# LoRA router on one core: x as float32 on SyncE's queue and float32 transposes, in place of a converting load on GpSimd's queue

## Chip, core and metric

The kernel runs on one NeuronCore of a Trainium2 chip. The metric is the device time of one execution in microseconds (us); the median of the runs shown counts. The engines are named as the profile has them: PE (TensorE's matmuls), PEld (TensorE's weight loads), DVE (VectorE), ACT (ScalarE), POOL (GpSimd), SP (SyncE); SP, ACT and POOL also issue DMA transfers.

## What is computed

```python
batch, seq, dim, num_loras = 16, 512, 1024, 8      # x, router_weights: float32
logits = np.matmul(x, router_weights)
exp_logits = np.exp(logits - np.max(logits, axis=-1, keepdims=True))
return (exp_logits / np.sum(exp_logits, axis=-1, keepdims=True)).astype(np.float32)
```

There are 8192 rows of 1024 values (33.5 MB of float32), a projection of each row onto 8 columns, and a softmax over these 8. Reading x once is nearly all of the memory traffic.

## The kernel before

x is taken as 64 blocks (MO) of 128 consecutive rows; a block has one row per partition and KO = 8 pieces of 128 columns. For each block:

- L62: POOL issues a DMA that reads 512 KB of float32 and writes 256 KB of bf16 into `x_bf`; the conversion is made in the transfer. `x_bf` has 6 buffers (L52), so the issue for block j waits until the transposes of block j - 6 have read theirs.
- L72: eight transposes on PE, each with a weight load (the 128 x 128 piece of `x_bf`) and a matmul against the bf16 identity, into one PSUM tile `pt` (2 buffers).
- L73: DVE copies `pt` (128 x 1024 bf16) to `xT` in SBUF.
- L77: eight projections on PE accumulate 128 x 8 logits in PSUM, each with a weight load (a piece of `xT`).
- L84: DVE copies the logits to `logits_sb`.

After each 8 blocks (MB) the softmax follows on 128 x 64 values: maximum and subtraction on DVE (L87, L89), exponential on ACT (L96), sum, reciprocal and product on DVE (L98 to L102), and SP issues the store (L108). In the result eight consecutive float32 values belong to one row and the rows of a partition lie 128 rows apart, so a store of 32 KB is 1024 pieces of 32 bytes.

The order of the instructions on each engine is the scheduler's: on PE the transposes of block j + 1 stand ahead of the projections of block j. Before the loop the identity is built on POOL (L43) and the weights are loaded by SP and converted by DVE (L45, L50).

Of the kernel before, what the change touches and what calls it, by code (L numbers as in the profile page):

```python
# [1 line left out]

# [5 lines left out]


@with_exitstack  # L10
def kernel(
    ctx: ExitStack,
    tc: tile.TileContext,
    x: bass.AP,
    router_weights: bass.AP,
    out: bass.AP,
):
    nc = tc.nc
    P = 128
    B, S, D = x.shape  # L20
    D2, N = router_weights.shape
    assert D2 == D
    M = B * S
    assert D % P == 0
    KO = D // P
    assert M % P == 0
    MO = M // P

    MB = 8
    assert MO % MB == 0  # L30
    MG = MO // MB

    x_flat = x.rearrange("b s d -> (b s) d")
    out_flat = out.rearrange("b s n -> (b s) n")

    fp32 = mybir.dt.float32
    bf16 = mybir.dt.bfloat16
    Exp = mybir.ActivationFunctionType.Exp
    X = mybir.AxisListType.X

    const_pool = ctx.enter_context(tc.tile_pool(name="const", bufs=1))
    identity = const_pool.tile([P, P], bf16)
    make_identity(nc, identity)  # L43
    w_f32 = const_pool.tile([P, KO, N], fp32)
    nc.sync.dma_start(  # L45
        out=w_f32[:],
        in_=router_weights.rearrange("(ko ki) n -> ki ko n", ki=P),
    )
    w_tile = const_pool.tile([P, KO, N], bf16)
    nc.vector.tensor_copy(out=w_tile[:], in_=w_f32[:])  # L50

    sbuf = ctx.enter_context(tc.tile_pool(name="sbuf", bufs=6))  # L52
    sm_pool = ctx.enter_context(tc.tile_pool(name="sm", bufs=3))
    psum_l = ctx.enter_context(tc.tile_pool(name="psum_l", bufs=2, space=bass.MemoryType.PSUM))
    psum_t = ctx.enter_context(tc.tile_pool(name="psum_t", bufs=2, space=bass.MemoryType.PSUM))

    for mg in range(MG):
        logits_sb = sm_pool.tile([P, MB, N], fp32)
        for mb in range(MB):
            mo = mg * MB + mb  # L60
            x_bf = sbuf.tile([P, KO, P], bf16)
            nc.gpsimd.dma_start(  # L62
                out=x_bf[:],
                in_=x_flat[mo * P:(mo + 1) * P, :].rearrange(
                    "m (ko ki) -> m ko ki", ki=P
                ),
            )

            xT = sbuf.tile([P, KO, P], bf16)
            pt = psum_t.tile([P, KO, P], bf16)  # L70
            for ko in range(KO):
                nc.tensor.transpose(pt[:, ko, :], x_bf[:, ko, :], identity)  # L72
            nc.vector.tensor_copy(out=xT[:], in_=pt[:])  # L73

            logits = psum_l.tile([P, N], fp32)
            for ko in range(KO):
                nc.tensor.matmul(  # L77
                    logits,
                    lhsT=xT[:, ko, :],
                    rhs=w_tile[:, ko, :],  # L80
                    start=(ko == 0),
                    stop=(ko == KO - 1),
                )
            nc.vector.tensor_copy(out=logits_sb[:, mb, :], in_=logits)  # L84

        mx = sm_pool.tile([P, MB, 1], fp32)
        nc.vector.reduce_max(mx[:, :, 0], logits_sb[:], axis=X)  # L87
        sub = sm_pool.tile([P, MB, N], fp32)
        nc.vector.tensor_tensor(  # L89
            out=sub[:],  # L90
            in0=logits_sb[:],
            in1=mx[:].broadcast_to([P, MB, N]),
            op=mybir.AluOpType.subtract,
        )
        expv = sm_pool.tile([P, MB, N], fp32)
        nc.scalar.activation(expv[:], sub[:], func=Exp)  # L96
        sm = sm_pool.tile([P, MB, 1], fp32)
        nc.vector.reduce_sum(sm[:, :, 0], expv[:], axis=X)  # L98
        inv = sm_pool.tile([P, MB, 1], fp32)
        nc.vector.reciprocal(inv[:], sm[:])  # L100
        outv = sm_pool.tile([P, MB, N], fp32)
        nc.vector.tensor_tensor(  # L102
            out=outv[:],
            in0=expv[:],
            in1=inv[:].broadcast_to([P, MB, N]),
            op=mybir.AluOpType.mult,
        )
        nc.sync.dma_start(  # L108
            out=out_flat[mg * MB * P:(mg + 1) * MB * P, :].rearrange(
                "(mb p) n -> p mb n", p=P  # L110
            ),
            in_=outv[:],
        )


# [1 line left out]
_INS = ['x', 'router_weights']  # L117
_OUTS = [((16, 512, 8), 'float32')]


# [23 lines left out]
```

## Time and profile before

| | |
|---|---|
| time, three runs | 97.52, 96.8, 97.43 us; median 97.43 |
| span of the profiled execution | 95.1 us |
| own time of the profiled execution | not listed apart from the three runs; they lie 1.7 to 2.4 us above its span |
| mean granted TensorE clock | 0.642 |
| busy | PE 75.5, PEld 68.7, DVE 55.4, ACT 3.3, POOL 34.6 us |
| x's loads | 64 issues, 6.5 us (median) from issue to landing |
| stores | 8 issues, 13.2 us (median) from issue to landing, the queue in front of them included |
| chain that ended last | DMA 48%, PE 21%, issue 14%, POOL 9% of the span |

The span runs from the first to the last instruction of the profiled execution. The page cuts it into 40 slices of 2.4 us; each digit is the busy share in tenths, and in the row PEclk the clock that TensorE was granted, in tenths of full speed (9 also stands for full). A group of instructions is a line with its count, its busy time, the mean of one in ns, and behind the last bar the idle time of the engine ahead of these instructions and what ended most of it. In the timeline the columns are start, duration, engine, line, operation, output and inputs, and the count; the end of a matmul is modelled, so that a row of eight that ends at 58.91 has handed PE to the next instruction earlier.

### The profile page before, as it was taken

The numbers are of one execution on the slowest core, as the hardware profiler recorded it, in microseconds if no ns is written. First come the engines' busy times: TensorE is split into PE (matmuls) and PEld (weight loads), VectorE is DVE, ScalarE is ACT, GpSimd is POOL, SyncE is SP. The second block draws the span as 40 slices with busy tenths as digits, with TensorE's granted clock in tenths as the row PEclk, the third lists the DMA queues.
The fourth block names the chain that finished last, engine by engine and source line by source line (L and its number), as shares of the span: only waits on it lengthen the run. The fifth ranks groups of instructions, "written<-read, shape, count | busy, mean of one in ns | idle before, by whom it ended". The sixth has DMA issues, their size and how long they took to land.

```text
span 95.1 us, 2428 instructions
## 1 busy us (share of the span) xinstructions
PE 75.5 (79%) x1024; PEld 68.7 (72%) x1024; DVE 55.4 (58%) x169; ACT 3.3 (4%) x9; POOL 34.6 (36%) x70
## 2 busy tenths in 40 slices
PE   0048996579999999899998999899979997699500
PEld 0037985468888899788887888898879885698400
DVE  0023666647766765767556765586676657666630
ACT  5000000010001000000001000100001000100010
POOL 6922444424443334434344433344443345100000
PEclk9999999975555555555555555555555559655885
DMA  1799999999999999999999999999999999996001
GB/s 11 120 185 199 208 208 216 202 209 209 211 208 198 210 209 207 202 211 209 196 211 210 208 210 197 210 208 207 208 204 210 207 200 210 210 209 82 0 4 10
DMA packets 18586, 17.22 MB, mean 181 GB/s; under 512 B 10384, under 2 KB 10384, under 8 KB 18576
## 3 DMA queue, kind: packets, MB, share of 16 engines
q0 software_dynamic: 9216, 16.78, 95.2%
q1 hardware_dynamic: 9360, 0.30, 7.6%
q8 instruction: 8, 0.13, 0.5%
q14 instruction: 2, 0.02, 0.0%
HBM read 33.59 MB, written 0.26 MB: 356 GB/s over the span
## 4 chain that ended last, share of the span: by engine, by line
DMA 48%; PE 21%; issue 14%; POOL 9%; DVE 2%; POOLq 0%; ACT 0%; ACTq 0%
DMA x_bf<-in_x_dram 48%; PE pt L72 17%; POOL x_bf L62 9%; PE logits L77 4%; DVE xT L73 1%; POOL identity masks.py:199 0%; POOLq L62 0%; ACT expv L96 0%; DVE sub L89 0%; DVE sm L98 0%; DVE mx L87 0%; DVE outv L102 0%; DVE inv L100 0%; POOL identity masks.py:197 0%; DVE logits_sb L84 0%
## 5 line engine op out<-in xcount | busy, mean ns | idle before, releaser
L72 PE MATMUL pt<-identity,x_bf 128*128 128x128 bf16 x512 | 63.0, 300 | 12.9 <-DMA x_bf<-in_x_dram 11.4
L72 PEld LDWEIGHTS <-x_bf 128*128 128x128 bf16 x512 | 46.8, 135 | 17.9 <-DMA x_bf<-in_x_dram 13.5
L73 DVE COPY xT<-pt 128x1024 bf16<-128x1024 bf16 x64 | 44.1, 689 | 24.0 <-PE pt L72 23.5
L62 POOL DMA_DIRECT2D x_bf<-in_x_dram x64 | 34.0, 532 | 46.0 <-PE logits L77 35.5
L77 PEld LDWEIGHTS <-xT 128*128 128x128 bf16 x512 | 24.2, 111 | 3.1 <-DVE xT L73 2.4
L77 PE MATMUL logits<-w_tile,xT 128*128 128x8 bf16 x512 | 25.0, 172 | 1.4 <-DVE xT L73 1.4
L84 DVE COPY logits_sb<-logits 128x8 f32<-128x8 f32 x64 | 9.9, 154 | 8.6 <-PE logits L77 8.6
L96 ACT ACTIVATE expv<-sub 128x64 f32<-128x64 f32 x8 | 2.0, 256 | 86.8 <-DVE sub L89 86.8
L50 DVE CAST w_tile<-w_f 128x64 bf16<-128x64 f32 x1 | 0.2, 195 | 3.0 <-DMA w_f<-in_router_weights_dram 3.0
L98 DVE TENSOR_REDUCE sm<-expv 128x8 f32<-128x64 f32 x8 | 1.7, 210 | 0.4 <-ACT expv L96 0.4
L89 DVE TENSOR_TENSOR sub<-logits_sb,mx 128x64 f32<-128x64 f32 x8 | 1.8, 224 | 0.0
L102 DVE TENSOR_TENSOR outv<-expv,inv 128x64 f32<-128x64 f32 x8 | 1.8, 223 | 0.1
L87 DVE TENSOR_REDUCE mx<-logits_sb 128x8 f32<-128x64 f32 x8 | 1.7, 210 | 0.0
L100 DVE RECIPROCAL inv<-sm 128x8 f32<-128x8 f32 x8 | 1.6, 195 | 0.0
L96 ACT ACT_TABLE_LOAD x1 | 1.3, 1283 | 0.7 <-PEq L128 0.7
masks.py:199 POOL TENSOR_SCALAR_AFFINE_SELECT identity<-identity 128x128 bf16<-128x128 bf16 x1 | 0.3, 304 | 0.1
masks.py:197 POOL MEMSET identity<- 128x128 bf16 x1 | 0.2, 204 | 0.3 <-POOLq L128 0.3
L128 POOL MEMSET const-float32-0.0<- 128x1 f32 x1 | 0.1, 98 | 0.2 <-issue 0.2
L128 POOL MEMSET const-bfloat16-1.0<- 128x1 bf16 x1 | 0.1, 102 | 0.0
L128 POOL MEMSET const-uint8-127<- 128x1 uint8 x1 | 0.1, 102 | 0.0
L128 POOL MEMSET const-float32-1.0<- 128x1 f32 x1 | 0.1, 98 | 0.0
## 6 DMA issues: line engine op xcount, KB each, us to landing
x_bf<-in_x_dram POOLq DMA_DIRECT2D x64, 256.0 KB, 6.5
out_dram<-outv SPq DMA_DIRECT2D x8, 32.0 KB, 13.2
w_f<-in_router_weights_dram SPq DMA_DIRECT2D x1, 32.0 KB, 2.2
```

The lines of the kernel that those rows point to most:

```text
L62: nc.gpsimd.dma_start(out=x_bf[:], in_=x_flat[mo * P:(mo + 1) * P, :].rearrange("m (ko ki) -> m ko ki", ki=P),)
L72: nc.tensor.transpose(pt[:, ko, :], x_bf[:, ko, :], identity)
L73: nc.vector.tensor_copy(out=xT[:], in_=pt[:])
L77: nc.tensor.matmul(logits, lhsT=xT[:, ko, :], rhs=w_tile[:, ko, :], start=(ko == 0), stop=(ko == KO - 1),)
L84: nc.vector.tensor_copy(out=logits_sb[:, mb, :], in_=logits)
L87: nc.vector.reduce_max(mx[:, :, 0], logits_sb[:], axis=X)
L89: nc.vector.tensor_tensor(out=sub[:], in0=logits_sb[:], in1=mx[:].broadcast_to([P, MB, N]), op=mybir.AluOpType.subtract,)
L96: nc.scalar.activation(expv[:], sub[:], func=Exp)
L98: nc.vector.reduce_sum(sm[:, :, 0], expv[:], axis=X)
L100: nc.vector.reciprocal(inv[:], sm[:])
L102: nc.vector.tensor_tensor(out=outv[:], in0=expv[:], in1=inv[:].broadcast_to([P, MB, N]), op=mybir.AluOpType.mult,)
L128: nc = _bacc.Bacc("TRN2", target_bir_lowering=False, num_devices=1)
```

## The change

- x is loaded by SP as plain float32, 20 loads of 1, 1, 2, then 14 times 4, then 2, 1, 1 "rows"; a row here is a 128 x 1024 piece with one row of x on each partition. Partition p now holds the rows 64 p to 64 p + 63 of x, so that a load of 4 rows reads 16 KB in one piece per partition, and what was block j is now row j of every partition. The pool of loads has 11 buffers.
[...]
- The conversion to bf16 is made by the copy from `pt` to `xT`: by ACT for odd rows, by DVE for even ones.
- The logits of up to 8 rows stay in one PSUM tile (2 buffers) and the softmax reads them there; the copy to `logits_sb` is gone. The groups of the softmax are 7 times 8 rows, then 4, 2, 1, 1.
- The results of all rows lie in one SBUF tile `outv` and are stored by ACT in two transfers: rows 0 to 55 after the seventh group, rows 56 to 63 at the end. Each partition's part is one contiguous piece (1792 and 256 bytes).
- The weights are loaded by ACT. The order of instructions is written out: the transposes and the copy of row j, then the projections of row j - 1 (and the softmax, where a group ends).

There is still one weight load and one matmul per transpose (512 and 512), and the projections are as before. On DVE a group's five softmax operations stand behind the copy of the next group's first row; on ACT the exponential stands ahead of the copy of its second row. SP's first seven loads wait for nothing; each later one waits for the transfer eight back (the weights' is one of them) to have landed, and from the twelfth on for the transposes that free its buffer.

```diff
-            nc.gpsimd.dma_start(
-                out=x_bf[:],
-                in_=x_flat[mo * P:(mo + 1) * P, :].rearrange(
-                    "m (ko ki) -> m ko ki", ki=P
-                ),
-            )
-            xT = sbuf.tile([P, KO, P], bf16)
-            pt = psum_t.tile([P, KO, P], bf16)
-            for ko in range(KO):
-                nc.tensor.transpose(pt[:, ko, :], x_bf[:, ko, :], identity)
-            nc.vector.tensor_copy(out=xT[:], in_=pt[:])
...
-            nc.vector.tensor_copy(out=logits_sb[:, mb, :], in_=logits)
...
+    x_rows = x.rearrange("b s d -> (b s) d").rearrange("(p j) d -> p j d", p=P)
+    out_rows = out.rearrange("b s n -> (b s) n").rearrange("(p j) n -> p j n", p=P)
...
+    LOADS = [1, 1, 2] + [4] * 14 + [2, 1, 1]
+    GROUPS = [8] * 7 + [4, 2, 1, 1]
+    STORES = {6: (0, 56), len(GROUPS) - 1: (56, J)}
...
+    xpool = ctx.enter_context(tc.tile_pool(name="x", bufs=11))
+    xtp = ctx.enter_context(tc.tile_pool(name="xT", bufs=4))
+    psum_t = ctx.enter_context(tc.tile_pool(name="psum_t", bufs=3, space=bass.MemoryType.PSUM))
...
+        for i, r in enumerate(LOADS):
+            xb = xpool.tile([P, r, D], fp32, name="xb")
+            nc.sync.dma_start(out=xb[:], in_=x_rows[:, j0:j0 + r, :])
...
+            if k == GROUPS[g] - 1:
+                softmax(g)
...
+            if g in STORES:
+                lo, hi = STORES[g]
+                nc.scalar.dma_start(out=out_rows[:, lo:hi, :], in_=outv[:, lo:hi, :])
...
+        for j in range(J):
+            xb, k = x_of[j]
+            pt = psum_t.tile([P, KO, P], fp32, name="pt")
+            for ko in range(KO):
+                nc.tensor.transpose(pt[:, ko, :], xb[:, k, ko * P:(ko + 1) * P], identity[:])
+            xT = xtp.tile([P, KO, P], bf16, name="xT")
+            if j % 2:
+                nc.scalar.copy(xT[:], pt[:])
+            else:
+                nc.vector.tensor_copy(out=xT[:], in_=pt[:])
+            if pend is not None:
+                project(*pend)
+            pend = (j, xT)
+        project(*pend)
```

More of the change, by code (lines that the diff above doesn't have):

```diff
@@ L23 @@
     M = B * S
-    assert D % P == 0
     KO = D // P
[L26 to L34, printed above, removed]
+    J = M // P
+    x_rows = x.rearrange("b s d -> (b s) d").rearrange("(p j) d -> p j d", p=P)
+    out_rows = out.rearrange("b s n -> (b s) n").rearrange("(p j) n -> p j n", p=P)
     fp32 = mybir.dt.float32
@@ L39 @@
     X = mybir.AxisListType.X
[L41 to L47, printed above, removed]
-    )
-    w_tile = const_pool.tile([P, KO, N], bf16)
-    nc.vector.tensor_copy(out=w_tile[:], in_=w_f32[:])
-    sbuf = ctx.enter_context(tc.tile_pool(name="sbuf", bufs=6))
@@ L53 @@
-    sm_pool = ctx.enter_context(tc.tile_pool(name="sm", bufs=3))
-    psum_l = ctx.enter_context(tc.tile_pool(name="psum_l", bufs=2, space=bass.MemoryType.PSUM))
[L55 to L61, printed above, removed]
-            nc.gpsimd.dma_start(
-                out=x_bf[:],
-                in_=x_flat[mo * P:(mo + 1) * P, :].rearrange(
-                    "m (ko ki) -> m ko ki", ki=P
-                ),
-            )
-            xT = sbuf.tile([P, KO, P], bf16)
-            pt = psum_t.tile([P, KO, P], bf16)
-            for ko in range(KO):
-                nc.tensor.transpose(pt[:, ko, :], x_bf[:, ko, :], identity)
-            nc.vector.tensor_copy(out=xT[:], in_=pt[:])
-            logits = psum_l.tile([P, N], fp32)
+    ALU = mybir.AluOpType
@@ new lines @@
+    LOADS = [1, 1, 2] + [4] * 14 + [2, 1, 1]
+    GROUPS = [8] * 7 + [4, 2, 1, 1]
+    assert sum(LOADS) == J and sum(GROUPS) == J
+    STORES = {6: (0, 56), len(GROUPS) - 1: (56, J)}
+    const = ctx.enter_context(tc.tile_pool(name="const", bufs=1))
+    xpool = ctx.enter_context(tc.tile_pool(name="x", bufs=11))
+    xtp = ctx.enter_context(tc.tile_pool(name="xT", bufs=4))
+    sm = ctx.enter_context(tc.tile_pool(name="sm", bufs=2))
+    psum_t = ctx.enter_context(tc.tile_pool(name="psum_t", bufs=3, space=bass.MemoryType.PSUM))
@@ new lines, with project @@
+    psum_l = ctx.enter_context(tc.tile_pool(name="psum_l", bufs=2, space=bass.MemoryType.PSUM))
+    x_of = []
+    with tc.manual_schedule():
+        identity = const.tile([P, P], fp32)
+        w_f32 = const.tile([P, KO, N], fp32)
+        w_bf = const.tile([P, KO, N], bf16)
+        outv = const.tile([P, J, N], fp32)
+        nc.scalar.dma_start(
+            out=w_f32[:],
+            in_=router_weights.rearrange("(ko ki) n -> ki ko n", ki=P),
+        )
+        make_identity(nc, identity)
+        j0 = 0
+        for i, r in enumerate(LOADS):
+            xb = xpool.tile([P, r, D], fp32, name="xb")
+            nc.sync.dma_start(out=xb[:], in_=x_rows[:, j0:j0 + r, :])
+            x_of += [(xb, k) for k in range(r)]
+            j0 += r
+        nc.vector.tensor_copy(out=w_bf[:], in_=w_f32[:])
+        group_of = [(g, k) for g, n in enumerate(GROUPS) for k in range(n)]
+        first = [sum(GROUPS[:g]) for g in range(len(GROUPS))]
+        logits = {}
+        pend = None
+        def project(j, xT):
+            g, k = group_of[j]
+            if k == 0:
+                logits[g] = psum_l.tile([P, GROUPS[g], N], fp32, name="lg")
@@ L76 @@
             for ko in range(KO):
                 nc.tensor.matmul(
-                    logits,
+                    logits[g][:, k, :],
                     lhsT=xT[:, ko, :],
-                    rhs=w_tile[:, ko, :],
+                    rhs=w_bf[:, ko, :],
                     start=(ko == 0),
@@ L83 @@
                 )
-            nc.vector.tensor_copy(out=logits_sb[:, mb, :], in_=logits)
[L86 to L113, printed above, removed]
+            if k == GROUPS[g] - 1:
+                softmax(g)
@@ new lines, in softmax @@
+        def softmax(g):
+            n, a = GROUPS[g], first[g]
+            lg = logits.pop(g)
+            mx = sm.tile([P, n, 1], fp32, name="mx")
+            nc.vector.reduce_max(mx[:, :, 0], lg[:], axis=X)
+            ex = sm.tile([P, n, N], fp32, name="ex")
+            nc.vector.tensor_tensor(
+                out=ex[:], in0=lg[:], in1=mx[:].broadcast_to([P, n, N]), op=ALU.subtract
+            )
+            ev = sm.tile([P, n, N], fp32, name="ev")
+            nc.scalar.activation(ev[:], ex[:], func=Exp)
+            ssum = sm.tile([P, n, 1], fp32, name="ssum")
+            nc.vector.reduce_sum(ssum[:, :, 0], ev[:], axis=X)
+            inv = sm.tile([P, n, 1], fp32, name="inv")
+            nc.vector.reciprocal(inv[:], ssum[:])
+            nc.vector.tensor_tensor(
+                out=outv[:, a:a + n, :], in0=ev[:], in1=inv[:].broadcast_to([P, n, N]), op=ALU.mult
+            )
+            if g in STORES:
+                lo, hi = STORES[g]
+                nc.scalar.dma_start(out=out_rows[:, lo:hi, :], in_=outv[:, lo:hi, :])
```

## The prediction

> **What bounds the kernel now.** I read the page first (busy shares, the forty slices, the queues), then the groups of instructions, then PE's timeline in three places, last the end of the timeline. Of the page:
>
> ```profile
> span 95.1 us, 2428 instructions
> PE 75.5 (79%) x1024; PEld 68.7 (72%) x1024; DVE 55.4 (58%) x169; ACT 3.3 (4%) x9; POOL 34.6 (36%) x70
> PEclk9999999975555555555555555555555559655885
> DMA  1799999999999999999999999999999999996001
> q0 software_dynamic: 9216, 16.78, 95.2%
> q1 hardware_dynamic: 9360, 0.30, 7.6%
> HBM read 33.59 MB, written 0.26 MB: 356 GB/s over the span
> ```
>
> The DMA engines are full from the second slice to the end of the loads, nearly all with x on q0. q1 moves only 0.30 MB but takes 7.6%: the results leave in pieces of 32 bytes. PE looks nearly as full, and its clock is mostly at one half, so the question is which of the two sets the pace. Groups:
>
> ```profile
> L72 PE MATMUL pt<-identity,x_bf 128*128 128x128 bf16 x512 | 63.0, 300 | 12.9 <-DMA x_bf<-in_x_dram 11.4
> L73 DVE COPY xT<-pt 128x1024 bf16<-128x1024 bf16 x64 | 44.1, 689 | 24.0 <-PE pt L72 23.5
> L50 DVE CAST w_tile<-w_f 128x64 bf16<-128x64 f32 x1 | 0.2, 195 | 3.0 <-DMA w_f<-in_router_weights_dram 3.0
> L96 ACT ACTIVATE expv<-sub 128x64 f32<-128x64 f32 x8 | 2.0, 256 | 86.8 <-DVE sub L89 86.8
> ```
>
> And the timeline, at half clock, at full clock, and at the end:
>
> ```profile
> 57.88 1.03 PE L72 MATMUL pt<-identity,x_bf 128*128 128x128 bf16 x8
> 58.71 0.40 PE L77 MATMUL logits<-w_tile,xT 128*128 128x8 bf16 x8
> 58.95 0.69 DVE L73 COPY xT<-pt 128x1024 bf16<-128x1024 bf16 x1 [0.52 <-PE pt L72]
> 59.16 1.03 PE L72 MATMUL pt<-identity,x_bf 128*128 128x128 bf16 x8
> ...
> 16.27 0.62 PE L72 MATMUL pt<-identity,x_bf 128*128 128x128 bf16 x8 [0.44 <-DMA x_bf<-in_x_dram]
> 16.73 0.34 PE L77 MATMUL logits<-w_tile,xT 128*128 128x8 bf16 x8
> 17.55 0.62 PE L72 MATMUL pt<-identity,x_bf 128*128 128x128 bf16 x8 [0.47 <-DMA x_bf<-in_x_dram]
> ...
> 87.63 1.03 PE L72 MATMUL pt<-identity,x_bf 128*128 128x128 bf16 x8
> 91.64 0.37 SPq L108 DMA_DIRECT2D out_dram<-outv  x1
> ```
>
> At half clock eight transposes take PE 0.83 us (57.88 to 58.71). The eight projections behind them take 0.23: 0.40 less the 0.17 (their mean) by which the last outlasts its start. PE thus works 1.06 us of a pitch of 1.28 (57.88 to 59.16); at full clock it works 0.46 + 0.17 = 0.63 and the pitch stays (16.27 to 17.55), PE waiting for x_bf. The loads set the pace, at either clock. From 10.02 to 17.55, with no store between, six blocks take 1.255 us each: 512 KB read per block, 418 GB/s. From the first block (5.39) to the last (87.63) it is 82.24 / 63 = 1.305; the difference, 0.05 a block or 3.1 us, lies where results are stored.
>
> The three runs are 96.8 to 97.52 us. Which one was profiled is not said, so what lies around the span is 1.7 to 2.4 us; I add 2.3 (97.43 - 95.1).
>
> **The change, part by part.**
>
> *Loads.* Gone: 64 issues on POOL (34.0 us, beside the DMA; nobody waits for POOL otherwise) and the wait of each on one of six buffers. New: 20 issues on SP, each 0.43 us by the weights' issue, at most eight in flight, with eleven buffers of up to four rows: the queue stays full unless PE falls some 30 rows behind. The bytes read are the same, the bytes written to SBUF double, and no row shows whether the engines mind. Lower bound of the pitch 1.20 us (the stores gone, and the conversion's share too), upper 1.31 (as now, nothing gained); I take 1.255, the stretch without stores. The first x landed 4.1 us after its issue on POOL (1.27 to 5.39); the weights on SP landed 2.2 us after theirs. So the first row, 512 KB, lands at 0.74 + 2.1 + 1.2 = 4.0, and the last at 4.0 + 63 x 1.255 = 83.1. Rows 4 to 7 come as one load, at 4.0 + 7 x 1.255 = 12.8: until then PE has only four rows to do.
>
> *Transposes.* 512, as before, each with its own weight load, now in float32. Lower bound: bf16's 0.107 us each at half clock (0.83 over eight, nearly); upper: twice that, or weight load and matmul no longer overlapping, 0.21. I take 0.107: it is still one weight load and one matmul per transpose, and the number of columns is the same. [...]
>
> *Copies out of PSUM.* 64 of 0.69 become 32 on VectorE and 32 on ScalarE. VectorE: 195 ns for 64 elements and 689 for 1024 give 0.49 us for the 960 between; not less than 0.69, and with float32 at half that rate 0.195 + 0.99 = 1.18; I take 1.20. ScalarE: 0.69 if as quick as VectorE is now, 0.256 + 0.99 = 1.25 if as slow; I take 1.0. The 64 small copies of logits (9.9 us of DVE) go.
>
> *The loop that the copies make.* PE does the transposes of j+1, then waits for the copy of j, then projects j, then starts on j+2. Today a copy of 0.69 fits in. With VectorE the turn from j to j+2 is, at half clock: 1.03 transposes, 0.04 to the copy (58.91 to 58.95), 1.20, 0.05 to PE, 0.23 projection: 2.55 for two rows, 1.28 a row. At full clock 0.62 + 0.04 + 1.20 + 0.05 + 0.17 = 2.08, or 1.04. ScalarE's turns are 0.2 shorter and fit in. Once per eight rows softmax stands in the copies' way: VectorE's five operations of 0.2 us (1.1 in all) come between two of its copies, and ScalarE's next copy waits behind the exponential. I take 0.4 us net, 0.05 a row (from nothing to 1.1 us, 0.14 a row). So PE's pitch is 1.33 at half clock and 1.09 at full clock, against 1.255 for the loads: the clock decides. In the trace it rose three times, each time after 3.4 us in which PE was busy for 3.3 or more (10.0 to 13.4, 74.9 to 78.3, 85.1 to 88.5), though not after each such stretch, and fell when PE waited. Behind the loads PE now has rows in hand and only short waits, 2.55 us with one gap of some 0.4; I expect the clock to be up for more than half the time, mean pitch 1.20. [...]
>
> *The end.* The last three loads are 2, 1 and 1 rows. Row 56 lands, with its load of four, at 83.1 - 4 x 1.255 = 78.1. If PE is not behind by then, row 63 starts at 78.1 + 7 x 1.09 = 85.7; from row 4 on at pitch 1.20 it is 12.8 + 59 x 1.20 = 83.6, so it is not. Before, row 63 started at 87.63. From there to the store's issue it is 4.0 now (91.64 - 87.63); ScalarE's copy adds 0.3, row 62's softmax ahead of row 63's 0.5, and smaller tiles return 0.2: 4.6. Store and end are 3.5 now (95.1 - 91.64); with 128 pieces in place of 1024 I take 3.0. Sum: 85.7 + 4.6 + 3.0 = 93.3 us of span, 95.6 of time, 1.8 less than before.
>
> The casts of w, the table load of ScalarE (1.28 us, from 0.74) and the float32 identity lie before the first row; they are hidden by 2 us of its load, and would cost their own length if it came at once.
>
> **The rivals.**
>
> *B, half clock throughout* (slower). Place: the wait of each second projection for VectorE's copy. Price: 12.8 + 59 x 1.33 = 91.3 for row 63's start, + 7.6 = 98.9 of span, 101.2 of time. It decides once the mean pitch is above 1.27, since 12.8 + 59 x 1.27 + 7.6 = 95.3, today's span: when the clock is at half for more than three quarters of the time. For it: 23 slices, some 55 us, in one piece at half clock in the trace. Against it: those three rises, at the same load on PE.
>
> *C, float32 transposes cost twice* (slower). At full clock the transposes take 0.9 and the turn is about 1.06 + 0.04 + 1.20 + 0.05 + 0.17 = 2.52: 1.31 with softmax, 100 of time. At half clock, 1.7 + 0.23 = 1.93 and more: 12.8 + 59 x 1.95 + 8.5 = 136 of span, 139 of time. For it: no float32 row exists. Against it: one matmul per transpose.
>
> *D, the loads gain more* (faster). A pitch of 1.22 and copies 0.1 shorter: last row lands at 3.9 + 63 x 1.22 = 80.8, row 63 starts at 80.8 - 4.9 + 7 x 1.03 = 83.1, + 7.2 = 90.3 of span, 92.6 of time. For it: POOL's share of the queue goes. Against it: double the bytes written.
>
> *E, the loads gain nothing*: 1.31 gives 4.0 + 63 x 1.31 = 86.5, row 63 at 86.5 - 5.2 + 7.6 = 88.9, 96.5 of span, 98.8.
>
> **How the numbers follow.** A (the sum above) 0.42, B 0.25, C 0.13, D 0.15, E 0.05. A's own range is 94 to 97.5, of which a third is within 1%. One per cent, about what a measurement of this kernel can tell, is 96.5 to 98.4 us. Faster: 0.28 of A and D, 0.43. Same: 0.14 of A, 0.01 of B, 0.02 of E, 0.17. Slower: the rest, 0.40. Predicted is A, 95.6. The range takes in D down to 91.8 and B with C's short form up to 103; C's long form and the far ends of D stay out.
>
> **What would show it.** x's packets ending near 82.5 to 83.5 and DMA full up to there (loads right); a transpose start-to-start of about 0.107 or 0.056 us by clock (else C); VectorE's copies at 1.2 and ScalarE's at 1.0; PE waiting for xT rather than for x in the middle; the clock at 1.00 for more than half the slices (else B). A PE that waits for xb in most rows would say that the copy loop is not the limit at all; one that is ten or more rows behind the loads at the end would make the prediction wrong.

## The result and the profile after

The changed kernel is slower: 103.34 us (median of four executions, 102.31 to 103.76) against 97.47 for the kernel before in the same comparison, a ratio of 1.061 with a 95% interval from 1.055 to 1.068. In three of the kernels below some executions show a lower clock than the fastest and take 1.7 to 4.2% longer (in one of them 97.25 us at a mean clock of 0.763, against 95.64 at 0.859); the ratios here and below leave them out. The profiled execution took 103.76 us; its span is 101.9, 6.8 more than before. Those 6.8 arise before row 63: its transposes start at 95.18, where they started at 87.63 before (+7.55), and from there to the end it is 6.7 us in place of 7.5.

The page of the changed kernel, in the rows that answer to those shown of before:

```profile
span 101.9 us, 2332 instructions
PE 84.2 (83%) x1024; PEld 73.7 (72%) x1024; DVE 49.1 (48%) x88; ACT 35.4 (35%) x44; POOL 0.7 (1%) x6
...
PEclk9999966999999999999999999999999999859985
DMA  2999999999999999999999999999999810200000
...
q1 hardware_dynamic: 2880, 33.56, 77.9%
```

Two things have changed places. DMA was full up to the 36th of the 40 slices; now it is full up to the 32nd (the last of x lands at 82.5 us), so the loads no longer set the end. And PE's clock, at half for 24 slices before, is now full from 16.9 to 88.6 us. PE is faster and still later. The groups, with busy time and the mean of one in ns, then idle time before them and its cause:

```profile
L116 PE MATMUL pt<-identity,xb 128*128 128x128 f32 x512 | 73.9, 292 | 6.1 <-DMA xb<-in_x_dram 6.1
...
L121 DVE CAST xT<-pt 128x1024 bf16<-128x1024 f32 x32 | 39.2, 1224 | 40.7 <-PE pt L116 40.5
...
L119 ACT CAST xT<-pt 128x1024 bf16<-128x1024 f32 x32 | 32.2, 1007 | 43.7 <-PE pt L116 42.5
```

The copies are as forecast. PE lost only 6.1 us to x, 4.5 of it before the first row: it does not wait for loads in the middle. The 292 ns of a transpose say little, as matmuls overlap (eight take 1.07 us together); the spacing has to be read from the timeline. In the middle of the span (start, duration, and in brackets the idle time before the instruction and what ended it):

```profile
51.37 1.07 PE L116 MATMUL pt<-identity,xb 128*128 128x128 f32 x8
...
52.48 1.23 DVE L121 CAST xT<-pt 128x1024 bf16<-128x1024 f32 x1 [1.38 <-PE pt L116]
53.76 0.35 PE L80 MATMUL lg<-w_bf,xT 128*128 128x8 bf16 x8 [0.21 <-DVE xT L121]
53.98 1.07 PE L116 MATMUL pt<-identity,xb 128*128 128x128 f32 x8
```

This is one turn. Eight transposes take 1.07 us at full clock (0.62 in bf16 before), their starts 0.109 us apart (0.056 in bf16). VectorE starts at 52.48, 0.04 after they end; its copy of 1.23 holds back the projection until 53.76, 0.05 after the copy; the next row but one starts 0.22 later. From 51.37 to 53.98 it is 2.61 us for two rows, 1.305 a row, against 1.24 at which the loads come ((82.5 - 4.48) / 63, first transpose to last landing). The chain that ended last shows the same beat: three of VectorE's copies in it, each one softmax group of eight rows later:

```profile
31.48 1.23 DVE xT L121
...
41.98 1.23 DVE xT L121
...
52.48 1.23 DVE xT L121
```

10.50 us for eight rows is 1.3125 a row: four turns of 2.61, and 0.06 for the softmax. 51 rows, from row 6 at 17.27 to row 57 at 84.20, run at this pitch.

Both ends add to that. Rows 4 to 7 come as one load, PE waits 1.43 us for it, and two rows then run at half clock (0.50 from 13.5 to 16.9). Near the end there is a wait that no part of the prediction has (ACTq is an issue on ScalarE's queue):

```profile
13.47 1.93 PE L116 MATMUL pt<-identity,xb 128*128 128x128 f32 x8 [1.43 <-DMA xb<-in_x_dram]
...
86.67 0.35 ACTq L110 DMA_DIRECT2D out_dram<-outv  x1
87.12 1.01 ACT L119 CAST xT<-pt 128x1024 bf16<-128x1024 f32 x1 [1.23 <-DVE outv L105]
88.19 0.35 PE L80 MATMUL lg<-w_bf,xT 128*128 128x8 bf16 x8 [1.64 <-ACT xT L119]
88.40 1.80 PE L116 MATMUL pt<-identity,xb 128*128 128x128 f32 x8
```

ScalarE's queue holds the first store (L110), which waits for VectorE's last softmax result; ScalarE's copy of a row stands behind it and starts 1.2 us late, PE waits 1.64 us for that copy, the clock falls (0.50 from 88.6 to 92.0), and the next eight transposes take 1.80 us. No run takes this wait out by itself. Against a pitch of 1.3125, rows 4 and 5 cost 1.2 us more (3.80 for two), and rows 57 to 62 3.1 more (10.98 for six).

### The profile page after: what moved, and what is told of

Same layout as the page of the kernel before. It is cut to its first block, busy times and chain, and to the rows that moved or that the text cites. A ratio compares the mean times of both kernels' runs of the same rounds, so it can differ in the third digit from the quotient of the medians.

```text
span 101.9 us, 2332 instructions
## 1 busy us (share of the span) xinstructions
PE 84.2 (83%) x1024; PEld 73.7 (72%) x1024; DVE 49.1 (48%) x88; ACT 35.4 (35%) x44; POOL 0.7 (1%) x6
## 4 chain that ended last, share of the span: by engine, by line
PE 46%; DVE 22%; ACT 13%; DMA 11%; issue 4%; SPq 1%; ACTq 0%
PE pt L116 35%; DVE xT L121 17%; ACT xT L119 12%; DMA xb<-in_x_dram 11%; PE lg L80 11%; DVE ex L96 2%; SPq L65 1%; DVE mx L94 1%; ACT ev L100 1%; DVE ssum L102 1%; DVE outv L105 1%; DVE inv L104 1%; ACTq L110 0%; ACTq L119 0%; ACTq L100 0%
## 5 line engine op out<-in xcount | busy, mean ns | idle before, releaser
L116 PE MATMUL pt<-identity,xb 128*128 128x128 f32 x512 | 73.9, 292 | 6.1 <-DMA xb<-in_x_dram 6.1
L116 PEld LDWEIGHTS pt<-identity,xb 128*128 128x128 f32 x512 | 59.6, 149 | 6.4 <-issue 5.9
L121 DVE CAST xT<-pt 128x1024 bf16<-128x1024 f32 x32 | 39.2, 1224 | 40.7 <-PE pt L116 40.5
L119 ACT CAST xT<-pt 128x1024 bf16<-128x1024 f32 x32 | 32.2, 1007 | 43.7 <-PE pt L116 42.5
L80 PEld LDWEIGHTS <-xT 128*128 128x128 bf16 x512 | 18.7, 97 | 17.7 <-ACT xT L119 8.9
L80 PE MATMUL lg<-w_bf,xT 128*128 128x8 bf16 x512 | 22.7, 168 | 7.5 <-ACT xT L119 4.7
L100 ACT ACTIVATE ev<-ex 128x64 f32<-128x64 f32 (+3 forms) x11 | 2.7, 242 | 18.6 <-DVE ex L96 18.5
L102 DVE TENSOR_REDUCE ssum<-ev 128x8 f32<-128x64 f32 (+3 forms) x11 | 2.2, 201 | 3.5 <-ACT ev L100 3.5
L105 DVE TENSOR_TENSOR outv<-ev,inv 128x64 f32<-128x64 f32 (+3 forms) x11 | 2.3, 206 | 0.4
L96 DVE TENSOR_TENSOR ex<-lg,mx 128x64 f32<-128x64 f32 (+3 forms) x11 | 2.3, 206 | 0.4
```

Source lines behind the costliest of these rows:

```text
L80: nc.tensor.matmul(logits[g][:, k, :], lhsT=xT[:, ko, :], rhs=w_bf[:, ko, :], start=(ko == 0), stop=(ko == KO - 1),)
L96: nc.vector.tensor_tensor(out=ex[:], in0=lg[:], in1=mx[:].broadcast_to([P, n, N]), op=ALU.subtract)
L100: nc.scalar.activation(ev[:], ex[:], func=Exp)
L102: nc.vector.reduce_sum(ssum[:, :, 0], ev[:], axis=X)
L105: nc.vector.tensor_tensor(out=outv[:, a:a + n, :], in0=ev[:], in1=inv[:].broadcast_to([P, n, N]), op=ALU.mult)
L116: nc.tensor.transpose(pt[:, ko, :], xb[:, k, ko * P:(ko + 1) * P], identity[:])
```

## The experiments

In the expectations, T is the theory that the turn sets the pace: transposes twice as long, a copy of 1.2 us, and a projection behind them, with only two rows on the way. R and S are the rivals: that PE's own float32 work sets it whatever the order, and that the late start with its half clock does. Times are medians; ratios are to the kernel before.

**Two rows between transposes and projection.** The smallest edit that breaks the turn and leaves PE's work as it is.

```diff
-            if pend is not None:
-                project(*pend)
-            pend = (j, xT)
-        project(*pend)
+            pend.append((j, xT))
+            if len(pend) > 2:
+                project(*pend.pop(0))
+        for p in pend:
+            project(*p)
```

> The changed kernel with the projections two rows behind the transposes in place of one. Theory T (the turn): in the changed kernel PE is held at every second row by VectorE's copy; a turn of two rows is 1.07 (transposes) + 0.04 + 1.23 (copy) + 0.05 + 0.22 (projection) = 2.61 us, 1.31 a row. With one more row between copy and projection the turn is no longer on the path: PE's pitch falls to the loads' 1.22 us or a little below while it catches up, row 63 starts at 86 to 88 in place of 95, span 93 to 95 us. Rival R (work): the float32 transposes themselves fill PE, pitch stays at 1.3, span 101 to 102. Rival S (start and end): the loss lies before row 8 and at the end, span 100 or more.

Measured: 95.74 us, ratio 0.984 (0.981 to 0.988), 7.6 us below the changed kernel. Its waits (total us, times, longest) and its timeline in the middle:

```profile
PE pt L116 <- DMA xb<-in_x_dram: 11.8, 15, 4.5
```

```profile
51.12 1.07 PE L116 MATMUL pt<-identity,xb 128*128 128x128 f32 x8
...
52.23 1.07 PE L116 MATMUL pt<-identity,xb 128*128 128x128 f32 x8
```

The transposes still take 1.07, but a row now takes 1.11 where x is there, and PE waits for x 15 times instead of 3. Row 63 starts at 86.19. The turn was the limit; PE's float32 work by itself is not, and the start, which is the same here, is not either.

**Each copy cut in two, half on VectorE and half on ScalarE.** It shortens the copy within the turn, with one row of lag.

```diff
-            if j % 2:
-                nc.scalar.copy(xT[:], pt[:])
-            else:
-                nc.vector.tensor_copy(out=xT[:], in_=pt[:])
+            H = KO // 2
+            nc.vector.tensor_copy(out=xT[:, :H, :], in_=pt[:, :H, :])
+            nc.scalar.copy(xT[:, H:, :], pt[:, H:, :])
```

> The changed kernel with every row's copy cut in two: VectorE takes the first four pieces, ScalarE the other four, at the same time. Theory T: each copy lasts about 0.7 us in place of 1.22, the turn is 1.07 + 0.04 + 0.70 + 0.05 + 0.22 = 2.08 for two rows, below the loads' 2.45, so the loads set the pitch: span 93 to 95 us as with the later projection. Rival R: 101 to 102. Rival S: 100 or more.

Measured: 106.95 us, ratio 1.100 (1.093 to 1.107): slower than the changed kernel, and the gain that T expects did not come. Waits and timeline of this kernel:

```profile
ACT xT L120 <- DVE xT L119: 58.3, 55, 4.7
```

```profile
51.22 0.69 DVE L119 CAST xT<-pt 128x512 bf16<-128x512 f32 x1 [0.91 <-PE pt L116]
51.94 0.59 ACT L120 CAST xT<-pt 128x512 bf16<-128x512 f32 x1 [0.96 <-DVE xT L119]
```

ScalarE starts its half only when VectorE's ends: the two write one tile, and the second waits for the first. Together they take 1.31 us (51.22 to 52.53) in place of 1.23. A longer copy made a longer time, which the turn explains; but the edit was no test of the shorter copy.

**The same with two PSUM tiles and two xT tiles.**

```diff
+            pt = [psum_t.tile([P, H, P], fp32, name=f"pt{h}") for h in range(2)]
...
+            xT = [xtp.tile([P, H, P], bf16, name=f"xT{h}") for h in range(2)]
+            nc.vector.tensor_copy(out=xT[0][:], in_=pt[0][:])
+            nc.scalar.copy(xT[1][:], pt[1][:])
```

> The copies cut in two once more, now with two PSUM tiles and two xT tiles per row, so that ScalarE's half does not wait for VectorE's as it did in the first attempt. Theory T (the turn): copy 0.69 at most, and the first half can start when four transposes are done; the turn is 1.07 + 0.04 + 0.69 + 0.05 + 0.22 = 2.07 us for two rows or less, below two loads (2.45): span 93 to 95 us. Rival R (PE's float32 work): 101 to 102.

Measured: 95.5 us, ratio 0.982 (0.977 to 0.988). Its waits:

```profile
ACT xT L120 <- PE pt L117: 46.2, 63, 4.1
...
PE pt L117 <- DMA xb<-in_x_dram: 10.0, 10, 4.7
```

ScalarE now waits for PE and no longer for VectorE, and PE for x. A second way of shortening the turn, with the order untouched, brings the same time as the longer lag. Which of the two tiles made the halves wait for each other was not tried apart.

**Float32 alone undone.** GpSimd converts on loading, as before; order, copies on two engines, loads of four rows and stores stay as in the changed kernel.

```diff
-        identity = const.tile([P, P], fp32)
+        identity = const.tile([P, P], bf16)
...
-            xb = xpool.tile([P, r, D], fp32, name="xb")
-            nc.sync.dma_start(out=xb[:], in_=x_rows[:, j0:j0 + r, :])
+            xb = xpool.tile([P, r, D], bf16, name="xb")
+            nc.gpsimd.dma_start(out=xb[:], in_=x_rows[:, j0:j0 + r, :])
...
-            pt = psum_t.tile([P, KO, P], fp32, name="pt")
+            pt = psum_t.tile([P, KO, P], bf16, name="pt")
```

> The changed kernel with the float32 part alone undone: GpSimd issues the same 20 loads with the conversion to bf16 in them, identity, transposes and PSUM tile are bf16. Theory T: transposes are 0.056 or 0.107 us by the clock, VectorE's copy 0.69, ScalarE's about 1.0; the turn is 2.1 to 2.3 for two rows at half clock and 1.9 at full clock, under two loads; span 91 to 94 us, faster than before by 1 to 4 us since the stores are large and the start early. Rival S, that the new order, groups and loads cost the time whatever the type: 98 or more.

Measured: 96.2 us, ratio 0.988 (0.983 to 0.993); span 94.3, just over what T named. VectorE's copy is 691 ns again, ScalarE's stays at 1009 with bf16. In this order float32 thus costs 7.1 us (103.34 - 96.2), and the rest of the change by itself gains 1.2%.

**Float32 alone, in the kernel before.** Loads by SyncE, float32 identity, xT still copied by VectorE alone.

```diff
-    identity = const_pool.tile([P, P], bf16)
+    identity = const_pool.tile([P, P], fp32)
...
-            x_bf = sbuf.tile([P, KO, P], bf16)
-            nc.gpsimd.dma_start(
+            x_bf = sbuf.tile([P, KO, P], fp32)
+            nc.sync.dma_start(
...
-            pt = psum_t.tile([P, KO, P], bf16)
+            pt = psum_t.tile([P, KO, P], fp32)
```

> The kernel before with the float32 part alone done: SyncE loads float32, identity, transposes and PSUM tile are float32, all else (VectorE alone copies, 6 buffers, small stores) as before. Theory T: VectorE now takes 1.22 + 0.15 (logits) + 0.17 (its share of softmax) = 1.54 us a row, more than PE's turn of 1.31 allows and more than the loads' 1.25; pitch 1.5 to 1.6, span 104 to 110 us. Rival R: PE alone, 1.3 a row, span 98 to 100. If the pitch were the loads' as before: 95.

Measured: 122.7 us in the profiled execution, span 120.7 (the others 121.2 to 126.3, no interval). More than expected: VectorE is busy for 88.8 us, as all 64 copies of 1.22 are its own, and on top of that the loads run dry. Page and SyncE's own waits:

```profile
GB/s 26 362 422 415 404 396 414 423 209 377 399 343 201 379 312 94 385 421 410 273 46 327 337 414 285 12 265 402 415 312 132 312 419 417 129 153 210 0 0 11
```

```profile
SPq L108 <- DVE logits_sb L84: 31.3, 5, 6.9
...
SPq L108 <- DVE outv L102: 17.9, 3, 10.6
```

The small stores (L108) stand on SyncE's queue among the loads, which SyncE did not have before. A store waits for its softmax, the loads behind it wait too, and the stream falls to 94, 46, 12 GB/s once per group. The changed kernel has nothing of this on SyncE's queue: its two stores are on ScalarE's queue and its copies on two engines. The shares of the two were not separated.

**Transposes of 64 columns.** What doubled: the pass of the data, or the loading of weights? This kernel transposes only 64 of each 128 rows, from 64 partitions, and its time has no meaning; the eight transposes at the start do. First the changed kernel, then this one:

```profile
4.48 3.64 PE L116 MATMUL pt<-identity,xb 128*128 128x128 f32 x16 [4.48 <-DMA xb<-in_x_dram]
```

```profile
4.85 1.09 PE L118 MATMUL pt<-identity,xb 64*128 64x64 f32 x8 [4.85 <-DMA xb<-in_x_dram]
```

> A look at the price of one float32 transpose. Only the first 64 partitions of x are transposed, projected and stored (half of the rows is left out; their results are zeros): each transpose has the same weight load of 128 columns, but its matmul streams 64 columns of the identity in place of 128. In the changed kernel transposes start 0.109 us apart at full clock, twice bf16's 0.056. If the matmul of float32 streams at half rate, the distance falls to about 0.055 to 0.06; if it is the weight load that takes 0.109, it stays at 0.11.

In the matmuls' rows the first pair is the stationary operand (partitions * columns), the second the moving one: the weights keep their 128 columns, the moving identity has 64 in place of 128. By its spacing the changed kernel is at half clock here (the page's clock row has no record before its first change): single transposes start 0.214 us apart. Here it is 0.107, at the start and to the end.

That rests on the clock here, of which this trace has no record. The weight loads tell it (duration in ns: shortest, median, longest), in the changed kernel at the start and in its middle, at full clock, then all of this kernel:

```profile
L116 PEld LDWEIGHTS pt<-identity,xb x16: 182/226/229, 4.4 to 7.5; 128*128 128x128 f32 x16
```

```profile
L116 PEld LDWEIGHTS pt<-identity,xb x64: 138/140/143, 49.9 to 60.0; 128*128 128x128 f32 x64
```

```profile
L118 PEld LDWEIGHTS pt<-identity,xb x512: 178/221/227, 4.8 to 106.8; 64*128 64x128 f32 x171
```

At full clock 0.107 would be the changed kernel's 0.109 unchanged, and would speak for the weight load; but no load here is shorter than 178 ns, where at full clock they last 140 in the changed kernel, so by its loads this kernel was at half clock throughout. Half the moving columns, half the time (0.107 for 0.214), with as many columns of weights: that fits the pass of the moving data as what takes twice as long in float32. A weight load that goes by partitions, of which there are also half, does not fit: by the records the loads last as long as before (221 against 226). No run halves the columns alone, so this is the author's reading.

**Finer loads at the start, one row of lag.**

```diff
-    LOADS = [1, 1, 2] + [4] * 14 + [2, 1, 1]
+    LOADS = [1] * 4 + [2] * 2 + [4] * 13 + [2, 1, 1]
```

> The changed kernel with its first loads smaller: four of 1 row and two of 2 ahead of those of 4, so that rows 4 to 7 arrive at 9 to 13 us one by one or in pairs and not together at 13.4. Theory T: PE starts on them some 3 us earlier, at half clock at first, and from then on keeps its 1.31 a row to the end, so the span falls by 2 to 4 us, to 98 to 100, and stays slower than before. Rival S (all that is lost is lost at the start): 95 or less.

Measured: 102.7 and 103.39 us in the two executions of four that the ratio takes in, 1.060 (1.051 to 1.069): the same as the changed kernel. Both theories missed. The start was not worth what either put on it.

**Finer loads, two rows of lag.** The same edit of LOADS on top of the first experiment.

> The later projection and the smaller first loads together. Theory T: with the later projection the loads set the pitch and the last landing the end, so the earlier start is worth nothing more: span 93.5 to 94.5, as with the later projection alone (94.0). Rival S: the 2 to 4 us of the start come off here too, 90 to 92.

Measured: 95.7 us, ratio 0.984 (0.978 to 0.991), span 93.9: with the lag, too, the finer start brings nothing. PE's timeline shows where it went:

```profile
15.11 1.07 PE L116 MATMUL pt<-identity,xb 128*128 128x128 f32 x8
...
20.05 1.94 PE L116 MATMUL pt<-identity,xb 128*128 128x128 f32 x8 [3.69 <-DMA xb<-in_x_dram]
...
22.05 1.56 PE L116 MATMUL pt<-identity,xb 128*128 128x128 f32 x8
...
23.65 1.07 PE L116 MATMUL pt<-identity,xb 128*128 128x128 f32 x8
```

PE does the early rows at once, then waits 3.69 us for the first load of four, and the clock falls for some 3.4 us (0.50 from 19.7 to 23.1). The wait is only moved from 13 to 20 us. With one row of lag the profiled execution, which the ratio leaves out, has the same wait (3.20 us, until 20.02); that it stands in the two others too is likely, not shown.

**Finer loads and groups at the end as well, two rows of lag.** A version that should beat both kernels.

```diff
-    LOADS = [1] * 4 + [2] * 2 + [4] * 13 + [2, 1, 1]
-    GROUPS = [8] * 7 + [4, 2, 1, 1]
+    LOADS = [1] * 4 + [2] * 2 + [4] * 11 + [2] * 3 + [1] * 6
+    GROUPS = [8] * 7 + [4, 2, 2]
```

> The later projection (lag 2), with both ends made finer: loads of 1, 1, 1, 1, 2, 2, then eleven of 4, three of 2 and six of 1; the softmax groups end with 4, 2, 2 in place of 4, 2, 1, 1. With the later projection alone the last x lands at about 83 us, but row 63 starts at 86.2, since rows 56 to 59 come as one load at 78 and PE needs 1.11 a row from there. Theory T: now the rows land one by one and PE follows them, row 63 starts at 83.5, and one softmax chain of 1.2 us less stands at the end: span 90 to 91.5 us, time 92 to 93.5, about 5% under the kernel before. If PE and not the landing sets the end: 93 or more.

Measured: 93.65 us, ratio 0.962 (0.959 to 0.965); span 91.8, just above the 90 to 91.5 that T named. Row 63's transposes start at 85.07, later than the 83.5 expected, since PE still catches up:

```profile
83.96 1.07 PE L116 MATMUL pt<-identity,xb 128*128 128x128 f32 x8
...
85.07 1.07 PE L116 MATMUL pt<-identity,xb 128*128 128x128 f32 x8
```

**The same with conversion on loading and bf16 transposes** (the edit of "float32 alone undone").

> The same kernel with the converting loads on GpSimd and bf16 transposes: the headline change undone with all else equal. If the loads set the pace in both, float32 costs nothing once its copies are off the path: the two are within 1 us; the float32 one a little ahead, since its stream ended at 82.5 to 82.8 and the converting one at 83.6 in the first runs, and its first row lands 1.5 us earlier. If PE's float32 work still costs: the bf16 one ahead by 2 us or more.

Measured: 92.33 us, ratio 0.947 (0.945 to 0.950), the best of all. Its last two rows:

```profile
82.77 0.62 PE L116 MATMUL pt<-identity,xb 128*128 128x128 bf16 x8 [0.45 <-DVE ex L96]
...
84.08 0.62 PE L116 MATMUL pt<-identity,xb 128*128 128x128 bf16 x8 [0.51 <-DMA xb<-in_x_dram]
```

Here PE waits for row 63 and starts it at 84.08, though x ends later (83.7, against 82.7 with float32). At 1.11 us a row float32 gains on loads of 1.24 by only 0.13 a row, so what PE fell behind is not made up by the end; and the last eight transposes take 0.45 longer. With everything else equal float32 costs 1.3 us here (93.65 - 92.33), where it cost 7.1 with one row of lag. That lies between the two expectations, and float32 is not ahead. SyncE's stream ends 1 us earlier, which does not pay for it; nor is it quicker: both bring a row in 1.24 us (first transpose to last landing, over 63), and the converting one's first transpose starts 0.9 later (5.44 against 4.53).

## Why the prediction was wrong

*The step that failed* is the transposes: "I take 0.107: it is still one weight load and one matmul per transpose, and the number of columns is the same." That is half clock; at full clock the step used 0.62 for eight. Measured: 0.214 us at half clock and 0.109 at full, the upper bound of twice bf16's value that stood in the same paragraph. The number of instructions and columns was right; the time differs with the type (0.109 in float32, 0.056 in bf16, 128 columns each), and no row of before could show that. The choice between the bounds rested on counting instructions, which says nothing on how long one takes. The run with 64 columns speaks for the moving data, and not for the weight load, as what takes longer (0.107 us for 0.214, with loads of 221 ns against 226).

*The loop* had the right form. The turn at full clock was put at 2.08 and is 2.61: 0.45 of the difference is the transposes, 0.05 the projection (0.22 for 0.17), 0.03 the copy. With 1.305 a row instead of 1.04 it passes the loads' pitch, and the copies, forecast at 1.20 and 1.0 and measured at 1.224 and 1.007, come to lie on the path. Softmax was put at 0.05 a row and takes 0.01 (0.06 per eight).

*The clock* was forecast up for more than half the time. It was full for 71.7 us in one piece, from 16.9 to 88.6, with the transposes as most of PE's work (over the span 73.9 us busy, against 22.7 for the projections). The mean pitch of 1.20 mixed 1.33 and 1.09; the pitch at full clock alone is 1.3125. The prediction's "23 slices" at half clock are 24 in its row, some 57 us; nothing else hangs on that. Had the clock stayed at half, rival C's long form of 139 us would have been near: by its sum a row is 1.95, and the four at half clock that no wait splits took 1.81 to 1.99.

*Rival C* is what happened, at 0.13 of the chances: "the turn is about ... 2.52: 1.31 with softmax, 100 of time." The pitch is right to 0.003, and that is luck: C's turn is 0.09 short (2.52 for 2.61), and the softmax in it about as much too long (0.10 for 0.015 in two rows). The time is 103.8 in the profiled execution, since C kept A's ends: rows 4 and 5 at half clock cost 1.2, the wait behind the store on ScalarE's queue with the half clock after it 3.1, the later load of rows 4 to 7 0.7 (13.47 for 12.8), the pitch 0.1 over 59 rows; what follows row 63's start and lies around the span gave back 1.3. 100.0 + 5.1 - 1.3 = 103.8. The range ended at 103.0: it held C at its own price and 3 us more, but not the ends as they came with it, the wait behind the store above all, which the prediction did not look for.

*The loads* were right: the last of x at 82.5 (82.5 to 83.5 was named), the first row at 4.48 for 4.0. The pitch, 1.24 for 1.255, is of no use while the turn is longer. *The end*: from row 63's transposes to the store's issue 4.4 (4.6), from there 2.35 (3.0).

*The copies* were priced right and the casts of the weights stayed hidden, as said. With the turn broken the forecast comes back: the first experiment's row 63 at 86.19, its time 95.74, stand beside 85.7 and 95.6. The sum was a sum for the kernel with a turn that fits. That it fits so closely is luck in part: the 1.09 a row behind the last load of four was bf16's turn with softmax, the measured 1.11 is PE's own float32 work.

## What to carry to other kernels

Price a transpose by its type and columns, not by its instruction count (one weight load and one matmul took 0.109 us in float32 and 0.056 in bf16 here), and where the trace has no such row, give the bound that reaches the next limit a real chance. A copy that gets longer matters by the turn it stands in (transposes, copy and consumer, divided by the rows on the way), not by its engine's busy share (48% for VectorE here); one more row between copy and consumer costs a few lines and was worth 7.6 us here. Before a store goes on an engine's queue, look what compute or loads stand behind it: here a copy started 1.2 us late, and a stream of loads fell to 12 GB/s.

## What the runs showed of the hardware

- Float32 transposes of 128 columns start 0.109 us apart at full clock and 0.214 at half, bf16 ones 0.056 and 0.107. 64 columns from 64 partitions in float32: 0.107, at half clock by its weight loads.
- With float32 the clock was full for 71.7 us of one span (mean 0.951); with bf16 in the kernel before it was mostly at half (mean 0.642), with PE busy for 79% against 83%. Waits of 1.4 to 3.7 us were followed by half clock for some 3.4 us. In the kernel with 64 columns the spacing stayed at 0.107 to the end, with PE busy for 89%: the clock seems never to have risen there (its trace has no clock record; this is inferred from the spacing and from its weight loads of 178 ns and more). What decides is open.
- ScalarE takes 1.01 us for a copy of 1024 elements per partition out of PSUM, from float32 and from bf16; VectorE takes 1.22 and 0.69.
- Two engines that write halves of one tile did so one after the other (VectorE from 51.22, 0.69 us long, ScalarE from 51.94, 0.59 long); with tiles of their own they ran side by side (VectorE from 50.07, 0.69 long, ScalarE from 50.56, 0.58 long).
- In loads of the same sizes 512 KB came in 1.24 us, as float32 on SyncE's queue ((82.7 - 4.53) / 63) and converted on GpSimd's ((83.7 - 5.44) / 63). The 1.255 of the kernel before is for loads of one row.
